# Two orders changed in a hybrid trunk kernel: weight blocks ahead of x's tiles in round 1, the bank ahead of its copy in output pair 1

## The chip, the cores and the metric

The kernel runs on one core of a Trainium2 chip. The metric is the device time of one launch in microseconds (us). Three runs of the kernel before gave a median of 867.38 us, 866.9 to 867.75. The engines are TensorE (PE), VectorE (DVE), ScalarE (ACT), GpSimd (POOL) and SyncE (SP), which issues most of the DMAs.

## The reference

One decoder layer. 2048 rows of x and 16 learned rows, 1024 wide, are normalised; one projection gives eight groups of 512 columns; four feed a gated short convolution, four a chunked retention with four heads; both halves are multiplied by an output matrix, added to the input rows and normalised again.

```python
def mixer_layer(h, norm_g, w_in, conv_w, ret_norm_g, w_out, pos):
    hn = rms_norm(h, norm_g)
    proj = jnp.einsum('bld,de->ble', hn, w_in)
    cx, cb, cc, cg, q, k, v, rg = jnp.split(proj, N_PROJ, axis=-1)
    conv_out = short_conv_branch(cx, cb, cc, conv_w) * jax.nn.silu(cg)
    qf = rotary(q.reshape(shp), pos) * (RET_HEAD_DIM ** -0.5)
    kf, vf = rotary(k.reshape(shp), pos), v.reshape(shp)
    ret = head_group_norm(retention_chunkwise(qf, kf, vf), ret_norm_g)
    ret_out = ret * jax.nn.silu(rg)
    mixed = jnp.concatenate([conv_out, ret_out], axis=-1)
    return h + jnp.einsum('ble,ed->bld', mixed, w_out)

h = mixer_layer(concat(meta, x), ...)
return rms_norm(h, final_g)[:, N_META:]
```

## The kernel before

The two large products, x by the input matrix and the mixed rows by the output matrix, are nearly all of PE's work. Each is cut into block products of 128x128 stationary by 128x512 moving. Every fp32 operand is split in two: a rounded high part (`mh` for the moving operand, `wh` for the stationary one), cast by ACT, and the rest (`ml`, `wl`), a subtraction on DVE. `split` (L116) writes this pair of instructions and keeps the last DVE one in `lowered`. A block product is then three matmuls: high by low, low by high, high by high.

A *quad* takes 2 by 2 blocks. `quad` (L235) forms it with seven products of 12 matmuls, 0 to 6, in three PSUM banks, by the recursion that saves one product in eight. Product 0, and then 2, 4 and 6 build up in the first bank, 1 in the second, 3 and 5 in the third. Between products ACT copies a bank to SBUF (`tc`, L253): the first bank after product 0, again after product 2 (this copy is called u2), and the third after product 3. A product that goes on in a copied bank waits for the copy, or for whoever took the bank. The four results are handed to a function `take(i, j, bank, copy)`: (0, 0) after product 1, (1, 1) after 4, (0, 1) after 5, and (1, 0), which has no copy, after 6. The sums of weight blocks that the recursion needs are made by POOL (L128, L131; tiles `sa` and `ra`).

`quad_plain` (L292) forms a quad with eight products and no sums; its matmuls have line L303. It is used at the start of round 1 (the first quad over x's second 1024 rows, beginning near 360 us) and in output pair 0. In round 1 its stationary operands, in the program's wording the weights' blocks, are cast as `mh30` to `mh33`, from `ra`; x's tiles are `mh00` to `mh13` (first half) and `mh70` to `mh73`, cast with a gain (L122, and L123 on DVE), from `x`. `moving` (L177) runs over x's tiles and splits them.

The outputs are made by pairs of 128-row tiles; pairs 1 and up use `quad`. Their `take` (L950) adds the residual rows, which stand in `yo`: with a copy, first `yo += copy` (on DVE in pair 1, on POOL in later pairs), then `yo = bank + yo` on DVE (L961), which is what frees the bank. Then ACT squares and sums the row (L964, L968), POOL multiplies two of the four quarters by the final gain (L972), and when both quarters of a row are there, DVE and POOL form the factor (L339, L342) and ACT and DVE scale (L993, L996).

The instructions of an engine run in the program's order on it. That order is not the source's: a scheduler sets it from the tiles' dependencies and a timing model, and the source steers it by `tc.issue_after(instruction)`, which places what is issued inside it behind that instruction. `queued` (L110) does so for several.

Of the kernel before, what the change touches and what calls it, by code (L numbers as in the profile page):

```python
# [13 lines left out]
ALU = mybir.AluOpType  # L14
# [5 lines left out]
KT = D // P  # L20
# [6 lines left out]
KH = KT // 2  # L27
# [6 lines left out]
FIRST_W, PLAIN_W, B12 = 2, 3, 4  # L34
# [44 lines left out]
def hybrid_trunk(ctx: ExitStack, tc: tile.TileContext, t, out: bass.AP, chunk_decay):  # L79
# [5 lines left out]
    nc = tc.nc  # L85
# [15 lines left out]
    def gen(name="g"):  # L101
        return sb.tile([P, HB + 16], F32, name=name, tag="g", bufs=GEN)[:, : 2 + HB]
# [1 line left out]
    def brief(name="b"):  # L104
        return sb.tile([P, HB + 128], F32, name=name, tag="b", bufs=BRIEF)[:, :HB]

    lowered, third, fifth, given = [None], [None], [None], [None, None]

    @contextmanager
    def queued(instructions):  # L110
        with ExitStack() as order:
            for ins in instructions:
                order.enter_context(tc.issue_after(ins.ins))
            yield

    def split(hi, lo, src, scale=None, eng=nc.vector):  # L116

        if scale is None:
            nc.scalar.copy(out=hi, in_=src)  # L119
            lowered[0] = eng.tensor_tensor(out=lo, in0=src, in1=hi.bitcast(F32), op=ALU.subtract)  # L120
            return
        scaled[0] = nc.scalar.mul(hi, src, scale)  # L122
        nc.vector.scalar_tensor_tensor(  # L123
            out=lo, in0=src, scalar=scale, in1=hi.bitcast(F32), op0=ALU.mult, op1=ALU.subtract
        )

    def add(eng, out, a, b):
        eng.tensor_tensor(out=out, in0=a, in1=b, op=ALU.add)  # L128
# [34 lines left out]
    def operand(i, kt):  # L163
        slot = B12 if i == 7 else i
        hi = sb.tile([P, HB], F32R, name=f"mh{i}{kt}", tag=f"mh{slot}{kt}", bufs=1)
        lo = sb.tile([P, HB], F32R, name=f"ml{i}{kt}", tag=f"ml{slot}{kt}", bufs=1)
        return hi, lo

    def parts(m, i, kt, src, factor=None):
        hi, lo = operand(i, kt)  # L170
        split(hi, lo, src, factor)
        m[i].append((hi, lo))
# [3 lines left out]
    def moving(load, scale=None, after={}, behind={}):  # L176


        m = [[] for _ in range(8)]
        blocks = []  # L180
        for j in range(2):
            for half in range(2):
                for kt in range(KH):
                    k = half * KH + kt
                    blocks.append(load(k, j))
                    with tc.issue_after(behind[j, k]().ins) if (j, k) in behind else nullcontext():
                        parts(m, BLOCK[half][j], kt, blocks[-1], scale(k) if scale else None)
                    after.get((j, k), lambda: None)()
        return m, blocks
# [91 lines left out]
    def plain_part(n, load, slot):  # L281
        a = sb.tile([P, HB], F32, name="ra", tag="ra", bufs=RAW)
        load(a)
        hi, lo = operand(slot, n)
        split(hi, lo, a)
        return a, (hi, lo)

    def plain_parts(loads, slot=PLAIN_W):
        w = {n: plain_part(n, loads[n], slot)[1] for n in (0, 2, 1, 3)}
        return [w[n] for n in range(4)]  # L290
# [167 lines left out]
    def load_x(r):  # L458
        def load(k, j):
            a = gen("x")[:, :HB]  # L460
            if r == 0:
                in_line(a, t["xT"][r, j, k])
            else:
                nc.sync.dma_start(a, t["xT"][r, j, k])
            return a

        return load
# [73 lines left out]
    def w_loads(n):  # L541
        return [lambda a, i=i: nc.sync.dma_start(a, t["w_in"][n, i]) for i in range(4)]
# [384 lines left out]
    def output(pair, m, final_g):  # L927
        d = mixed[pair // 2]
        loads = [
            lambda a, i=i, k=k: nc.sync.dma_start(a.rearrange("p (k c) -> p k c", k=KH), d[pair % 2, i, k])  # L930
            for i in range(2)
            for k in range(2)
        ]
        ys = [[None, None], [None, None]]
        ss = small.tile([P, 2, 3], F32, name="so", tag="so")
        cuts = [1, 1]
        for i in range(2):
            for j in range(2):
                y = gen("yo")[:, :HB]
                row = (2 * pair + i) * P  # L940
                nc.sync.dma_start(y, x[row : row + P, j * HB : (j + 1) * HB])
                ys[i][j] = y
        last = [None]
        squares = []

        def square():
            while squares:
                squares.pop(0)()

        def take(i, j, pp, c):  # L950
            y = ys[i][j]
            if c is not None:

                with tc.issue_after(fifth[0].ins) if pair == 1 and i + j == 0 else nullcontext():
                    add(nc.vector if pair == 1 else nc.gpsimd, y, y, c)
            junk = sb.tile([P, HB], F32, name="rot", tag="rot", bufs=1)

            cut = 2 if c is None and pair == SEQ // (2 * P) - 1 else 1
            for n in range(cut):
                cs = slice(n * HB // cut, (n + 1) * HB // cut)  # L960
                last[0] = nc.vector.tensor_tensor(out=y[:, cs], in0=pp[:, cs], in1=y[:, cs], op=ALU.add)  # L961
                at = ss[:, i, 2 * n : 2 * n + 1] if i != j and n else ss[:, i, j : j + 1]
                if pair and i + j == 0:
                    squares.append(lambda cs=cs, at=at: nc.scalar.activation(  # L964
                        junk[:, cs], y[:, cs], AF.Square, accum_out=at
                    ))
                else:
                    nc.scalar.activation(junk[:, cs], y[:, cs], AF.Square, accum_out=at)  # L968
            cuts[i] = cut
            if i == j:  # L970
                ys[i][j] = gen("z")[:, :HB]
                nc.gpsimd.tensor_tensor(out=ys[i][j], in0=y, in1=final_g[:, j * HB : (j + 1) * HB], op=ALU.mult)  # L972

        if pair == 0:
            w = plain_parts(loads)
            prepared(m, sums_w, (1, 3))
            quad_plain(w, m, take)
            prepared(m, sums_w, (0, 2), held)
        else:
            quad(stationary(load_raw(loads)), m, take, (idle, idle, square))  # L980
        for i in range(2):
            tot = small.tile([P, 1], F32, name="tot", tag="tot")
            add(nc.vector, tot, ss[:, i, 0:1], ss[:, i, 1:2])
            if cuts[i] > 1:
                add(nc.vector, tot, tot, ss[:, i, 2:3])
            rs = small.tile([P, 1], F32, name="rf", tag="rf")
            rsqrt_mean(rs, tot)
            row = (2 * pair + i) * P
            for j in range(2):
                cs = slice(j * HB, (j + 1) * HB)  # L990
                y = ys[i][j]
                if i == j:
                    nc.scalar.mul(y, y, rs)  # L993
                else:
                    with tc.issue_after(last[0].ins):
                        nc.vector.scalar_tensor_tensor(  # L996
                            out=y, in0=y, scalar=rs, in1=final_g[:, cs], op0=ALU.mult, op1=ALU.mult
                        )
                (nc.scalar if i == j and cuts[i] > 1 else nc.sync).dma_start(out[row : row + P, cs], y)
# [39 lines left out]
    for r in range(NR):  # L1039
# [7 lines left out]
        if r == 0:  # L1047
            w = [[None] * 4 for _ in range(2)]

            def begin(half):  # L1050
                if half:
                    for q, slot in enumerate((FIRST_W, PLAIN_W)):
                        for n in (1, 3):
                            w[q][n] = plain_part(n, lambda a: in_line(a, t["w_in"][2 * NG + q, n]), slot)
                    return
                for n in (0, 2):
                    fetch(1, n, PIECES[0])
# [17 lines left out]
            pieces = []  # L1075

            def meta_behind():
# [3 lines left out]
            after = {  # L1081
                (0, 0): lambda: (begin(0), split_pieces(0)),
                (0, 1): lambda: split_pieces(1),
                (0, KH - 1): lambda: begin(1),
                (0, KT - 1): lambda: (pieces.append(scaled[0]), meta_behind()),
            }
            m, b = moving(load_x(r), gain_of, after, {(0, k): lambda k=k: pieces[k > 1] for k in range(1, KH)})
            first = [[p for a, p in tiles] for tiles in w]
            blocks = None, meta_products([a for a, p in w[0]])
            with tc.issue_after(line[0].ins):  # L1090
# [26 lines left out]
            between = (), idle, idle, idle  # L1117
            later = prepare(load_x(1), sums_x, gain_of)
        else:
            m, b = moving(load_x(r), gain_of)  # L1120
            first = [plain_parts(w_loads(0))]
            load_tables()
            prepared(m, sums_x, (1, 3))

# [12 lines left out]
        for n, unit in enumerate(units):  # L1137
# [10 lines left out]
            else:  # L1148
                if r == NR - 1 and following is None:
                    lent = sb.tile([P, 2, BLK], F32, name="held", tag="rot_t", bufs=1)  # L1150
                    areas = [lent[:, 0], lent[:, 1], row_tile("held", 0), row_tile("held", 0)]
                    for i, a in enumerate(areas):
                        for j in range(2):
                            n, kt = 2 * (i // 2), i % 2 * 2 + j
# [7 lines left out]
    m, b = moving(load_w_out)  # L1162
# [42 lines left out]
```

## Time and profile before

| | |
|---|---|
| median of 3 runs | 867.38 us (866.9 to 867.75) |
| the profiled run's own time | 867.37 us |
| span of the profiled execution | 865.6 us |
| granted TensorE clock, mean | 0.997 of full speed |
| busy: PE, DVE, ACT, POOL | 854.3, 719.0, 499.1, 373.2 us |
| share of PE on the chain that ended last | 86% |

The span is what the trace covers. The run's own time is 1.77 us longer, which is what lies around it. The matmul at L246 alone, three forms of 1008, is 73% of the chain that ended last.

### The profile page before, as it was taken

Reading aid. Unit: us, or ns where it says so; the run is one execution under the profiler, and the core shown is the slowest. Engines: PE = TensorE matmul, PEld = TensorE weight load, DVE = VectorE, ACT = ScalarE, POOL = GpSimd, SP = SyncE. Lnnn points to the kernel's source line nnn. Section 1 sums busy time; section 2 is a strip of 40 time slices with the busy share of each in tenths; the row PEclk is TensorE's granted clock in tenths of the full one; section 3 lists DMA queues with packets and bytes.
Section 4 is the critical chain, followed back from the end, with each engine's and each line's share of the span. In section 5 each row is a group of like instructions: output and inputs, shape, how many; then the busy total and the mean of one; then the engine's idle time right before and its main releaser. Section 6 shows DMA issues by size and latency. Waiting matters only on the chain.

```text
span 865.6 us, 12697 instructions
## 1 busy us (share of the span) xinstructions
PE 854.3 (99%) x4216; PEld 705.0 (81%) x4216; DVE 719.0 (83%) x1204; ACT 499.1 (58%) x901; POOL 373.2 (43%) x278
## 2 busy tenths in 40 slices
PE   9999999999999999999999999999999999999996
PEld 6778888878887778788888888888888888788885
DVE  7788989888897977989789898988767799877663
ACT  8775648474855554948374757544433566545553
POOL 0023232423245554352242323354746555678773
PEclk9999999999999999999999999999999999999998
DMA  9714245454656633845263746646122484545431
GB/s 326 252 62 98 61 97 161 112 146 135 158 173 192 195 98 98 320 142 147 62 158 122 164 129 127 202 114 216 49 77 82 175 324 136 168 164 185 151 135 73
DMA packets 127506, 129.51 MB, mean 150 GB/s; under 512 B 58384, under 2 KB 76112, under 8 KB 127440
## 3 DMA queue, kind: packets, MB, share of 16 engines
q1 hardware_dynamic: 126864, 128.30, 49.7%
q8 instruction: 33, 0.54, 0.3%
q10 hardware_dynamic: 576, 0.40, 0.1%
q14 instruction: 33, 0.27, 0.1%
HBM read 90.91 MB, written 25.17 MB: 134 GB/s over the span
## 4 chain that ended last, share of the span: by engine, by line
PE 86%; DVE 6%; issue 2%; ACT 0%; POOL 0%; POOLq 0%; DVEq 0%
PE pj L246 73%; PE pj L303 5%; PE ms L886 2%; PE ms L875 2%; PE ms L885 2%; PE ms L862 2%; DVE wl L120 1%; PE ms L500 1%; DVE ml L120 1%; DVE yo L128 0%; DVE ml L123 0%; DVE yo L961 0%; PE pj L327 0%; DVE yo L996 0%; ACT n L442 0%
## 5 line engine op out<-in xcount | busy, mean ns | idle before, releaser
L246 PE MATMUL pj<-mh,wl 128*128 128x512 f32 x1008 | 395.9, 393 | 1.6 <-DVE wl L120 1.1
L246 PE MATMUL pj<-mh,wh 128*128 128x512 f32 x1008 | 393.2, 390 | 0.0
L246 PE MATMUL pj<-ml,wh 128*128 128x512 f32 x1008 | 392.7, 390 | 0.0
L119 ACT CAST wh<-ra 128x512 fp32r<-128x512 f32 x216 | 134.0, 620 | 232.5 <-PE pj L246 193.3
L120 DVE TENSOR_TENSOR wl<-ra,wh 128x512 fp32r<-128x512 f32 x216 | 192.4, 893 | 40.8 <-ACT wh L119 39.9
L246 PEld LDWEIGHTS pj<-mh,wl 128*128 128x128 f32 x1008 | 189.3, 188 | 43.1 <-issue 2.3
L246 PEld LDWEIGHTS pj<-mh,wh 128*128 128x128 f32 x1008 | 189.3, 188 | 39.5
L246 PEld LDWEIGHTS pj<-ml,wh 128*128 128x128 f32 x1008 | 189.3, 188 | 38.1
L131 POOL TENSOR_TENSOR ra<-ra 128x512 f32<-128x512 f32 x70 | 115.1, 1644 | 101.6 <-PE ms L500 51.3
L128 POOL TENSOR_TENSOR sa<-ra 128x512 f32<-128x512 f32 x35 | 52.7, 1505 | 102.3 <-DVE wl L120 39.8
L131 POOL TENSOR_TENSOR ra<-sa,ra 128x512 f32<-128x512 f32 x35 | 49.9, 1425 | 81.3 <-DVE wl L120 74.1
L253 ACT COPY tc<-pj 128x512 f32<-128x512 f32 x108 | 62.6, 580 | 0.1
L898 POOL TENSOR_TENSOR rp<-rs,neg_half 128x4 f32<-128x4 f32 x16 | 18.9, 1183 | 45.0 <-DVE rs L128 44.9
L961 DVE TENSOR_TENSOR yo<-pj,yo 128x512 f32<-128x512 f32 (+1 forms) x33 | 22.0, 671 | 16.2 <-PE pj L246 8.1
L972 POOL TENSOR_TENSOR z<-yo,final_g 128x512 f32<-128x512 f32 x16 | 26.8, 1674 | 18.6 <-DVE yo L961 18.6
L647 POOL TENSOR_TENSOR c<-c,rr 128x512 f32<-128x512 f32 x14 | 25.0, 1789 | 21.1 <-DVE c L688 11.1
L119 ACT CAST wh<-sa 128x512 fp32r<-128x512 f32 x36 | 22.2, 618 | 17.4 <-PE pj L246 17.1
L647 POOL TENSOR_TENSOR c<-c,tc 128x512 f32<-128x512 f32 x14 | 23.2, 1659 | 19.9 <-ACT tc L673 19.7
L128 DVE TENSOR_TENSOR tc<-pj,tc 128x512 f32<-128x512 f32 x28 | 19.2, 684 | 13.5 <-PE pj L246 13.3
L902 DVE TENSOR_SCALAR pm<-ms,mv,rp 128x128 f32<-128x128 f32 x64 | 21.8, 402 | 10.2 <-POOL rp L898 10.2
L123 DVE SCALAR_TENSOR_TENSOR ml<-x,gain,mh 128x512 fp32r<-128x512 f32 x32 | 25.2, 822 | 5.5 <-ACT mh L122 5.4
L120 DVE TENSOR_TENSOR wl<-sa,wh 128x512 fp32r<-128x512 f32 x36 | 28.9, 804 | 0.8 <-ACT wh L119 0.7
(161 smaller groups left out, 1256.0 us busy)
## 6 DMA issues: line engine op xcount, KB each, us to landing
ra<-in_w_in SPq DMA_DIRECT2D x124, 256.0 KB, 2.8
x<-in_xT SPq DMA_DIRECT2D x48, 256.0 KB, 4.9
w<-in_w_out SPq DMA_DIRECT2D x32, 256.0 KB, 4.5
ra<-mixed SPq DMA_DIRECT2D x32, 256.0 KB, 2.7
yo<-in_x SPq DMA_DIRECT2D x32, 256.0 KB, 4.9
ra<-in_x SPq DMA_DIRECT2D x16, 256.0 KB, 3.4
mixed<-c SPq DMA_DIRECT2D x16, 256.0 KB, 2.4
sums_x<-x SPq DMA_DIRECT2D x16, 256.0 KB, 2.8
```

The lines of the kernel that those rows point to most:

```text
L119: nc.scalar.copy(out=hi, in_=src)
L120: lowered[0] = eng.tensor_tensor(out=lo, in0=src, in1=hi.bitcast(F32), op=ALU.subtract)
L123: nc.vector.scalar_tensor_tensor(out=lo, in0=src, scalar=scale, in1=hi.bitcast(F32), op0=ALU.mult, op1=ALU.subtract)
L128: eng.tensor_tensor(out=out, in0=a, in1=b, op=ALU.add)
L131: eng.tensor_tensor(out=out, in0=a, in1=b, op=ALU.subtract)
L246: nc.tensor.matmul(bank, a[:, ks], b, start=first and kt == 0 and n == 0, stop=kt == KH - 1 and n == 2, skip_group_check=not first,)
L253: copied[0] = nc.scalar.copy(out=c, in_=bank)
L303: nc.tensor.matmul(banks[i], a[:, ks], b, start=half + kt + n == 0, stop=half == 1 and kt == KH - 1 and n == 2,)
L647: eng.tensor_tensor(out=out, in0=a, in1=b, op=ALU.mult)
L902: nc.vector.tensor_scalar(out=y[:, cs], in0=o[:, cs], scalar1=mv[:, c, 0:1], scalar2=rp[:, c, :], op0=ALU.subtract, op1=ALU.mult,)
L961: last[0] = nc.vector.tensor_tensor(out=y[:, cs], in0=pp[:, cs], in1=y[:, cs], op=ALU.add)
L972: nc.gpsimd.tensor_tensor(out=ys[i][j], in0=y, in1=final_g[:, j * HB : (j + 1) * HB], op=ALU.mult)
```

## The change

Two things are edited.

First, in round 1. Before, all of x's tiles were split (`moving`), and then the weights' four blocks. Now the parts of blocks 0 and 2 are written behind x's first tile, those of 1 and 3 behind its third, and every x tile but the first is queued behind the last cast and the last subtraction of the weight blocks. `split` keeps the cast in `raised` for that.

Second, in output pair 1, for the two quarters (1, 1) and (0, 1), which have a copy: `yo = bank + yo` comes first and `yo += copy` second. Quarter (0, 0) and all other pairs are as before. No operation is added or removed.

```diff
-    lowered, third, fifth, given = [None], [None], [None], [None, None]
+    lowered, raised, third, fifth, given = [None], [None], [None], [None], [None, None]
...
         if scale is None:
-            nc.scalar.copy(out=hi, in_=src)
+            raised[0] = nc.scalar.copy(out=hi, in_=src)
             lowered[0] = eng.tensor_tensor(out=lo, in0=src, in1=hi.bitcast(F32), op=ALU.subtract)
...
                     blocks.append(load(k, j))
-                    with tc.issue_after(behind[j, k]().ins) if (j, k) in behind else nullcontext():
+                    with queued(behind.get((j, k), list)()):
                         parts(m, BLOCK[half][j], kt, blocks[-1], scale(k) if scale else None)
...
             y = ys[i][j]
-            if c is not None:
+            late = pair == 1 and c is not None and i + j > 0
+            if c is not None and not late:
...
                 last[0] = nc.vector.tensor_tensor(out=y[:, cs], in0=pp[:, cs], in1=y[:, cs], op=ALU.add)
+                if late:
+                    last[0] = nc.vector.tensor_tensor(out=y, in0=y, in1=c, op=ALU.add)
...
-            m, b = moving(load_x(r), gain_of)
-            first = [plain_parts(w_loads(0))]
+            loads, w = w_loads(0), {}
+
+            def begin(ns):
+                for n in ns:
+                    w[n] = plain_part(n, loads[n], PLAIN_W)[1]
+
+            m, b = moving(
+                load_x(r), gain_of, {(0, 0): lambda: begin((0, 2)), (0, 2): lambda: begin((1, 3))},
+                {(j, k): lambda: [raised[0], lowered[0]] for j in range(2) for k in range(KT) if j + k},
+            )
+            first = [[w[n] for n in range(4)]]
             load_tables()
```

ACT at the start of round 1, before. `mh30` and its fellows are the weights' blocks, `mh00` to `mh13` x's tiles, `wh` a weight of the quad that runs before, `rr` row factors.

```order
L122 ACTIVATE mh10_3838<-x_3836,gain_69 128x512 [waits DMAHW6_49]
L119 CAST wh_3670<-ra_3639 128x512 [waits DVE_49,PE_49]
L253 COPY tc_3747<-pj_3678 128x512
L673 ACTIVATE tc_3691<-tc_3691 128x512 [waits DVE_49]
L122 ACTIVATE mh11_3844<-x_3842,gain_69 128x512 [waits DMAHW7_49]
L376 COPY rr_2929<-ms_3699 128x512 [waits PE_49]
L378 ACTIVATE rr2_2930<-ms_3699 128x512
L119 CAST mh30_3910<-ra_3908 128x512 [waits PE_49]
L122 ACTIVATE mh12_3850<-x_3848,gain_69 128x512 [waits DMAHW0_49]
L119 CAST mh31_3922<-ra_3920 128x512 [waits PE_49]
L122 ACTIVATE mh13_3856<-x_3854,gain_69 128x512 [waits DMAHW1_49]
L119 CAST mh32_3916<-ra_3914 128x512 [waits PE_49]
```

The same place now:

```order
L119 CAST wh_3666<-ra_3641 128x512 [waits PE_49,Activation_49]
L119 CAST wh_3670<-ra_3639 128x512 [waits DVE_49,PE_49]
L253 COPY tc_3747<-pj_3678 128x512
L673 ACTIVATE tc_3691<-tc_3691 128x512 [waits DVE_49]
L376 COPY rr_2929<-ms_3699 128x512 [waits PE_49]
L378 ACTIVATE rr2_2930<-ms_3699 128x512
L119 CAST mh30_3820<-ra_3818 128x512 [waits DMAHW6_49,PE_49]
L119 CAST mh31_3844<-ra_3842 128x512 [waits DMAHW0_49,PE_49]
L119 CAST mh32_3826<-ra_3824 128x512 [waits DMAHW7_49,PE_49]
L122 ACTIVATE mh01_3832<-x_3830,gain_69 128x512 [waits DMAHW3_49]
L122 ACTIVATE mh02_3838<-x_3836,gain_69 128x512 [waits DMAHW4_49]
```

The weights' casts moved ahead of x's tiles `mh01` to `mh11`.

DVE in output pair 1, before. `yo_7386` is quarter (1, 1), `tc_7489` its copy, `pj_7429` the first bank, `wl_7426` the low part that product 6 needs.

```order
L120 TENSOR_TENSOR wl_7422<-ra_7390,wh_7421 128x512 [waits Activation_49]
L128 TENSOR_TENSOR yo_7382<-yo_7382,tc_7474 128x512 [waits DMAHW2_49,Activation_49]
L120 TENSOR_TENSOR wl_7426<-ra_7394,wh_7425 128x512 [waits DMAHW4_49,Activation_49]
L128 TENSOR_TENSOR yo_7386<-yo_7386,tc_7489 128x512 [waits DMAHW4_49,Activation_49]
L961 TENSOR_TENSOR yo_7386<-pj_7429,yo_7386 128x512 [waits DVE_49,PE_49]
L120 TENSOR_TENSOR wl_7580<-ra_7570,wh_7579 128x512 [waits DMAHW3_49,Activation_49]
L961 TENSOR_TENSOR yo_7382<-pj_7476,yo_7382 128x512 [waits PE_49]
```

And now:

```order
L120 TENSOR_TENSOR wl_7422<-ra_7390,wh_7421 128x512 [waits Activation_49]
L120 TENSOR_TENSOR wl_7426<-ra_7394,wh_7425 128x512 [waits DMAHW4_49,Activation_49]
L962 TENSOR_TENSOR yo_7386<-pj_7429,yo_7386 128x512 [waits DMAHW4_49,PE_49]
L120 TENSOR_TENSOR wl_7580<-ra_7570,wh_7579 128x512 [waits DMAHW3_49,Activation_49]
L964 TENSOR_TENSOR yo_7386<-yo_7386,tc_7489 128x512 [waits DVE_49]
L962 TENSOR_TENSOR yo_7382<-pj_7476,yo_7382 128x512 [waits DMAHW2_49,PE_49]
```

Both additions of a copy moved behind the addition of the bank.

PE in the next pair, 2, whose source is not edited: the first rows of products 2, 3 and 4, before. `mh20` marks product 2, `mh30` product 3, `mh40` product 4; `pj_7611` is the first bank, `pj_7658` the third.

```order
L246 MATMUL pj_7611<-mh20_7165,wl_7592 128x512 [waits DVE_49,Activation_49]
L246 MATMUL pj_7611<-ml20_7166,wh_7591 128x512
...
L246 MATMUL pj_7658<-mh30_7327,wl_7596 128x512 [waits DVE_49]
L246 MATMUL pj_7658<-ml30_7328,wh_7595 128x512
...
L246 MATMUL pj_7611<-mh40_7343,wl_7600 128x512 [waits DVE_49,Activation_49]
```

And now:

```order
L246 MATMUL pj_7658<-mh30_7327,wl_7596 128x512 [waits DVE_49]
L246 MATMUL pj_7658<-ml30_7328,wh_7595 128x512
...
L246 MATMUL pj_7611<-mh20_7165,wl_7592 128x512 [waits Activation_49]
L246 MATMUL pj_7611<-ml20_7166,wh_7591 128x512
...
L246 MATMUL pj_7611<-mh40_7343,wl_7600 128x512 [waits DVE_49,Activation_49]
```

The scheduler has exchanged products 2 and 3, 12 matmuls each. ACT there, before and now, `tc_7656` being u2 of the first bank:

```order
L119 CAST wh_7603<-ra_7572 128x512 [waits DVE_49,PE_49]
L253 COPY tc_7656<-pj_7611 128x512
L119 CAST wh_7607<-ra_7576 128x512 [waits DMAHW0_49,DVE_49,PE_49]
L253 COPY tc_7671<-pj_7658 128x512
```

```order
L119 CAST wh_7603<-ra_7572 128x512 [waits DVE_49,PE_49]
L119 CAST wh_7607<-ra_7576 128x512 [waits DMAHW0_49,PE_49]
L253 COPY tc_7656<-pj_7611 128x512
L253 COPY tc_7671<-pj_7658 128x512
```

The cast of `wh_7607` moved ahead of the copy u2.

## Rows read from the trace of the kernel before

**Rows 1.** The page's part 1: busy us, share of the span, instructions.

```profile
PE 854.3 (99%) x4216; PEld 705.0 (81%) x4216; DVE 719.0 (83%) x1204; ACT 499.1 (58%) x901; POOL 373.2 (43%) x278
```

**Rows 2.** PE's waits: us in total, times, longest us.

```profile
PE pj L303 <- DVE ml L120: 1.0, 1, 1.0
...
PE pj L246 <- DVE yo L961: 0.5, 1, 0.5
```

**Rows 3.** Timeline of PE near 361 us: start, duration, instruction, [idle <-releaser].

```profile
360.00 0.39 PE L303 MATMUL pj<-mh,mh 128*128 128x512 f32 x1
361.40 0.50 PE L303 MATMUL pj<-mh,ml 128*128 128x512 f32 x1 [1.01 <-DVE ml L120]
```

**Rows 4.** Timeline of ACT, 353 to 359 us.

```profile
353.12 2.70 ACT L122 ACTIVATE mh<-x,gain 128x512 fp32r<-128x512 f32 x4 [0.39 <-DMA x<-in_xT]
...
357.25 0.71 ACT L122 ACTIVATE mh<-x,gain 128x512 fp32r<-128x512 f32 x1
...
358.81 0.62 ACT L119 CAST mh<-ra 128x512 fp32r<-128x512 f32 x1
```

**Rows 5.** Timeline of DVE, 354 to 361 us.

```profile
354.51 0.67 DVE L647 TENSOR_TENSOR tc<-tc,rr 128x512 f32<-128x512 f32 x1
...
360.67 0.68 DVE L120 TENSOR_TENSOR ml<-ra,mh 128x512 fp32r<-128x512 f32 x1
```

**Rows 6.** Timeline of DVE, 388 to 404 us, three of 18 rows.

```profile
388.70 0.69 DVE L709 TENSOR_TENSOR rot<-kv,rot_t 64x512 f32<-64x512 f32 x1 [2.27 <-ACT kv L766]
...
401.60 1.78 DVE L712 TENSOR_TENSOR qg<-qg,rot 128x512 f32<-128x512 f32 x1
403.31 0.68 DVE L128 TENSOR_TENSOR qg<-pj,tc 128x512 f32<-128x512 f32 x1
```

**Rows 7.** Timeline of PE at product 6 of the next quad.

```profile
404.83 0.39 PE L246 MATMUL pj<-mh,wl 128*128 128x512 f32 x1
```

**Rows 8.** Timeline of POOL, 382 to 403 us.

```profile
382.36 5.23 POOL L131 TENSOR_TENSOR ra<-ra 128x512 f32<-128x512 f32 x1 [6.02 <-issue]
387.55 1.28 POOL L647 TENSOR_TENSOR c<-c,tc 128x512 f32<-128x512 f32 x1
401.39 1.45 POOL L128 TENSOR_TENSOR sa<-ra 128x512 f32<-128x512 f32 x1 [12.55 <-DMA ra<-in_w_in]
```

**Rows 9.** Timeline of PE near 741 us, output pair 1.

```profile
740.34 0.39 PE L246 MATMUL pj<-mh,wh 128*128 128x512 f32 x1
741.24 0.50 PE L246 MATMUL pj<-mh,wl 128*128 128x512 f32 x1 [0.51 <-DVE yo L961]
741.57 0.39 PE L246 MATMUL pj<-ml,wh 128*128 128x512 f32 x1
```

**Rows 10.** Timeline of DVE, 739 to 741 us.

```profile
739.11 0.68 DVE L120 TENSOR_TENSOR wl<-ra,wh 128x512 fp32r<-128x512 f32 x1
739.71 0.68 DVE L128 TENSOR_TENSOR yo<-yo,tc 128x512 f32<-128x512 f32 x1
740.49 0.69 DVE L961 TENSOR_TENSOR yo<-pj,yo 128x512 f32<-128x512 f32 x1
```

**Rows 11.** Timeline of PE in pair 2: product 2's last matmul, first ones of 3 and 4.

```profile
752.02 0.39 PE L246 MATMUL pj<-mh,wh 128*128 128x512 f32 x1
752.25 0.39 PE L246 MATMUL pj<-mh,wl 128*128 128x512 f32 x1
...
754.97 0.39 PE L246 MATMUL pj<-mh,wl 128*128 128x512 f32 x1
```

**Rows 12.** Timeline of ACT behind product 2 of pair 2.

```profile
752.45 0.62 ACT L119 CAST wh<-ra 128x512 fp32r<-128x512 f32 x1 [2.10 <-PE pj L246]
752.98 0.58 ACT L253 COPY tc<-pj 128x512 f32<-128x512 f32 x1
```

**Rows 13.** Timeline of DVE, 748 to 752 us: a scaling, then product 3's low part.

```profile
748.93 1.87 DVE L996 SCALAR_TENSOR_TENSOR yo<-yo,rf,final_g 128x512 f32<-128x512 f32 x1 [0.66 <-POOL rf L342]
750.72 0.68 DVE L120 TENSOR_TENSOR wl<-sa,wh 128x512 fp32r<-128x512 f32 x1
```

More of the change, by code (lines that the diff above doesn't have):

```diff
@@ L1086, in hybrid_trunk @@
             }
-            m, b = moving(load_x(r), gain_of, after, {(0, k): lambda k=k: pieces[k > 1] for k in range(1, KH)})
+            m, b = moving(load_x(r), gain_of, after, {(0, k): lambda k=k: [pieces[k > 1]] for k in range(1, KH)})
             first = [[p for a, p in tiles] for tiles in w]
```

## The prediction

> **What bounds the kernel now.** I read the busy shares first: PE works 854.3 us of 865.6, 99%, and no other engine comes near [rows 1]. So a change pays only where PE waits, and costs only where it makes PE wait. The view of PE's waits comes second: behind the opening stretch, two of them are over 0.2 us, one at L303 for a subtraction and one at L246 for an addition of pair 1 [rows 2]. They are where the two edits apply. The timelines of PE then give what each takes. Matmuls start every 0.227 us when nothing holds them (12 of them from 752.25 to 754.97 [rows 11]).
>
> At 361.40 the start is 1.40 us behind the one before it, so 1.17 is lost [rows 3]; at 741.24 it is 0.90, so 0.67 is lost, and the matmul behind it starts 0.33 later and not 0.227, which is 0.11 more [rows 9]. I count this restart of 0.11 with every wait. Together, 1.28 + 0.78 = 2.06 us is the most that can be gained. That is 0.24% of the time; about 0.2%, 1.74 us, is what a measurement of this kernel can tell from no change.
>
> **Round 1, the wait itself.** No operation is added; the order on ACT changes. PE's matmul at 361.40 needs the low part that DVE begins at 360.67 [rows 5], and that one needs the cast that ACT begins at 358.81 [rows 4]. Before it ACT does five tiles of x (four at 353.12, one at 357.25) in the same stretch. Now none of them is between `wh_3670` and the first weight. What remains is bound by DVE: the row factor is multiplied at 354.51, ending 355.18 [rows 5], and behind it on ACT come the activation L673, two factor rows and the cast, at 0.5 us from one to the next (the cast of 752.45 is followed after 0.53 [rows 12]). The cast starts near 355.2 + 3 x 0.53 = 356.8, 2.0 us sooner, and the low part ends near 358.2 where PE wants it at 360.23. The other three weights follow at some 0.6 us each. The wait goes, with 2 us to spare, and so 1.28 us.
>
> **Round 1, what is late next.** PE now runs 1.28 us ahead, but DVE has the same operations to do. The place to look is where DVE has no gap: from 388.70 to 403.31 it works without one, through 18 rows [rows 6]. The last of these, `qg<-pj,tc` of the next quad, frees the first bank for product 6, which starts at 404.83 [rows 7]. It ends 403.31 + 0.68 = 403.99, so PE has 0.84 us to spare there. The chain starts at 388.70, behind ACT's copy of a bank of PE's, after 2.27 us of idle time. If it starts 1.28 sooner like PE, the margin stays and place one is worth the whole 1.28. If DVE's own backlog holds the start at 388.70, product 6 is 1.28 - 0.84 = 0.44 late, with the restart 0.55, and 0.73 is left. If one more meeting with POOL falls on the busy stretch, then 1.09 more (the op at 401.60 took 1.78 where its like takes 0.69 [rows 6], under POOL's addition from 401.39 to 402.84 [rows 8]): stall 1.64, and place one loses 0.36. The reason to expect something of that kind is that POOL's operation of 387.55 lies in DVE's idle time now [rows 6, 8]; when everything of PE's comes 1.28 sooner, that idle time shrinks to about 1.0 us and does not cover its 1.28. Against it, the meeting of 401.39 can move ahead of the chain's end without changing its cost. Laid out with the rows' durations, the new order has the chain start between 387.6 and 388.9; at the middle, 388.3, it is 0.4 sooner, and product 6 is 1.28 - 0.84 - 0.4, about nothing, late. With half a meeting to a whole one (0.55 to 1.09) and the restart that is 0.7 to 1.2. I take the middle, 0.94: place one is **-0.34**, between -1.28 and +0.36.
>
> The Trainium skill ("SBUF — State Buffer", section "Who interferes with whom") calls the port pair of DVE and GpSimd an exclusive lock, and says that whoever starts first holds it for the whole instruction. The 1.78 at 401.60 fits that; POOL's 5.23 us at 382.36, where DVE kept on issuing, shows POOL waiting through several of DVE's instructions rather than one [rows 8]. [...]
>
> **Pair 1.** The bank that product 6 waits for is freed at 741.18 by L961 (740.49 + 0.69), in front of which stands `yo<-yo,tc` of 739.71 [rows 10]. Now that addition comes behind. Even with the low part left at 739.11, L961 starts at 739.71 and ends 740.40, before 740.34 + 0.227 = 740.57, when PE is ready. The wait of 0.78 us goes: **-0.78**. The additions that are put later have the same length and DVE has idle time behind them; POOL and ACT get the quarter (1, 1) later, but PE does not wait for it.
>
> **Pair 2, which nobody edited.** The scheduler exchanges products 2 and 3. Product 4 goes on in product 2's bank, and must wait for the copy u2 of it. Before, product 3's 12 matmuls (2.72 us [rows 11]) stood between, and cast and copy were hidden: behind product 2's last matmul at 752.02 the cast starts at 752.45, the copy at 752.98, and it ends 753.56, well before 754.97 [rows 11, 12]. Now product 4 is next in PE's order, the cover is gone, and the cast of `wh_7607` stands ahead of the copy on ACT. From the last matmul to the first of product 4 it takes 753.56 - 752.02 = 1.54, plus about 0.05 for the signal, 1.59 in place of 0.227: 1.36, with the restart **+1.47**. Lower bound, if the copy goes first: without the cast's 0.53 it is 0.94. Upper bound: an ACT scaling or square in front, some 0.7 more, 2.2.
>
> Product 3 now also starts one product sooner, where product 2 starts now: 752.25 - 2.72 = 749.53, less 0.78 is 748.75. Its low part began at 750.72 before, behind a scaling of 1.87 us that met POOL [rows 13]. In the new order the two scalings stand directly in front of it. Their inputs come 0.78 sooner, with PE. Without the meeting (1.87 to 0.75, 1.1 less) the low part starts at 750.72 - 0.78 - 1.1 = 748.84; the sum and the factor of the second row now stand ahead of both scalings, which I put at 0.6 more; with its own 0.68 it ends at 748.9. That is 0.15 late, with the restart 0.26; between 0 and 1.4 (if the meeting remains). I take **+0.2**. Behind this PE has no wait to the end that could take the loss up, so pair 2 costs 1.67.
>
> **The sum.** -0.34 - 0.78 + 1.47 + 0.2 = +0.55. On the profiled run's own 867.37 us (its span of 865.6 with 1.77 around it, and the same as the median of 867.38) this is **867.9 us**. The rest of the edits (where DMAs of the weights stand against x's on SP, the later square of one quarter) I set at nothing: PE reads none of their results within 2 us.
>
> **The rivals.**
>
> *A. Both waits go and nothing new appears.* -2.06, 865.3 us. For it: both waits are real, and in the first place the margin is 2 us. Against: the exchange in pair 2 has a price read from rows, and the hardware keeps the order of each engine.
>
> *B. DVE falls behind and the bank comes late, slower than before.* Mechanism: PE's lead at 361 pulls POOL's operations onto DVE's busy stretch, DVE's chain to 403.99 gets one meeting more, and product 6 waits 1.64 us; in pair 2 the same happens in front of product 3's low part (+1.4 in place of 0.2). Sum: +0.36 - 0.78 + 1.47 + 1.4 = +2.45, 869.8 us; with the first alone +1.25, 868.6. It is measurably slower from about 1.7 us lost beyond the gain, which needs the second meeting nearly whole. For it: the 1.09 us of each meeting is in the rows; against: POOL must hit these places.
>
> *C. Round 1 keeps its whole 1.28.* DVE's chain starts as much sooner as PE. -1.28 - 0.78 + 1.67 = -0.39, 867.0 us. For it: DVE's idle 2.27 is larger than 1.28.
>
> *D. The edit in round 1 does nothing*, because the weights' tiles or a DMA hold the cast where it was. 0 - 0.78 + 1.67 = +0.9, 868.3 us. Against: ACT runs without a gap there.
>
> **How the numbers follow.** Forecast 0.48 (867.3 to 868.5), C 0.20, B 0.18, D 0.07, A 0.07. Only A with all of its 2.06 is faster by over 0.2%: 0.07. Slower needs +1.74: the upper part of B, 0.14, and 0.02 of the forecast with an upper bound on u2. Within 0.2%: 0.77. The range of 8 in 10 runs from C with the copy first (-0.9, 866.5) to B (869.2).
>
> **What would show it.** Round 1: no wait at the second L303 matmul, and the first weight's cast near 356.8. If product 6 of the next quad is not late, C holds; if it is late by over 1.5, B. Pair 1: no wait for L961 at product 6. Pair 2: a wait at the first matmul of product 4, released by ACT's copy at L253, of about 1.3 us idle between starts; and a short one, or none, at product 3. The forecast is wrong if there is no wait for L253, or if the new PE wait near 405 exceeds one microsecond.

## The result and the profile after

Measured: 869.35 us, median of 7 runs (868.35 to 871.03), against 867.36 us (866.38 to 867.75) of the kernel before. The ratio is 1.0028, 95% interval 1.0018 to 1.0037. The change makes the kernel 1.99 us slower. The forecast was 867.9 us with a range that ended at 869.2.

PE's waits in the trace after (us in total, times, longest us):

```profile
PE pj L246 <- DVE wl L120: 2.1, 4, 0.9
PE pj L246 <- DVE qg L128: 1.4, 1, 1.4
PE pj L246 <- ACT tc L253: 1.2, 1, 1.2
```

Both waits of [rows 2] that the edits aim at are gone. Two lines are new, one for DVE's `qg` and one for ACT's copy, and the waits for weights' low parts have grown (1.1 us before, over the whole run).

The profiled run is the slowest of the seven, 871.03 us, so its span of 869.2 must not be compared with 865.6 as it stands. It is read by stage: the lag of one matmul of PE behind the same one in the trace of before. The rows of after, in order of time:

```profile
361.54 0.39 PE L303 MATMUL pj<-mh,mh 128*128 128x512 f32 x1
361.76 0.39 PE L303 MATMUL pj<-mh,ml 128*128 128x512 f32 x1
...
404.83 0.39 PE L246 MATMUL pj<-mh,wh 128*128 128x512 f32 x1
406.61 0.50 PE L246 MATMUL pj<-mh,wl 128*128 128x512 f32 x1 [1.39 <-DVE qg L128]
...
750.60 0.39 PE L246 MATMUL pj<-mh,wh 128*128 128x512 f32 x1
751.53 0.50 PE L246 MATMUL pj<-mh,wl 128*128 128x512 f32 x1 [0.54 <-DVE wl L120]
...
756.92 0.39 PE L246 MATMUL pj<-mh,wh 128*128 128x512 f32 x1
758.50 0.50 PE L246 MATMUL pj<-mh,wl 128*128 128x512 f32 x1 [1.19 <-ACT tc L253]
```

| matmul | before | after | lag |
|---|---|---|---|
| first at L303 | 360.00 [rows 3] | 361.54 | 1.54 |
| second at L303 | 361.40 [rows 3] | 361.76 | 0.36 |
| product 6 of the next quad | 404.83 [rows 7] | 406.61 | 1.78 |
| first of the second product in pair 2 | 752.25 - 2.72 = 749.53 [rows 11] | 751.53 | 2.00 |
| product 4 of pair 2 | 754.97 [rows 11] | 758.50 | 3.53 |

The first 1.54 us lie ahead of both edits, where PE's matmuls are the same in both kernels: it is the variation of the opening from run to run. In e1 (below), which has the same edit there, this matmul starts at 359.64, 0.36 earlier than before. From there to product 4 the lag grows by 3.53 - 1.54 = 1.99 us, as much as the difference of the medians (2.12 with the restart behind that wait). So the loss lies at the places of the table: -1.18 at 361 us, +1.42 to product 6, +0.22 to pair 2 (in it pair 1's gain, the wait in front of product 3, a restart and some 0.2 at other places), then +1.53.

The wait at 361 is gone because ACT casts the first three weights from 358.34 on, with no tile of x ahead of them ([rows 4] had five in the same stretch):

```profile
357.85 0.61 ACT L378 ACTIVATE rr<-ms 128x512 f32<-128x512 f32 x1
358.34 1.67 ACT L119 CAST mh<-ra 128x512 fp32r<-128x512 f32 x3
```

358.34 - 1.54 is 356.80 on the clock of before, where the prediction put it.

At product 6 the chain on DVE is the cause. POOL and then DVE in the trace after, up to 406 us; they answer to [rows 6, 8]:

```profile
401.66 1.44 POOL L128 TENSOR_TENSOR sa<-ra 128x512 f32<-128x512 f32 x1 [18.46 <-DMA ra<-in_w_in]
403.18 1.63 POOL L131 TENSOR_TENSOR ra<-ra 128x512 f32<-128x512 f32 x1
```

```profile
390.33 0.69 DVE L709 TENSOR_TENSOR rot<-kv,rot_t 64x512 f32<-64x512 f32 x1
...
401.25 0.69 DVE L120 TENSOR_TENSOR wl<-ra,wh 128x512 fp32r<-128x512 f32 x1
401.86 1.79 DVE L711 TENSOR_TENSOR qg<-qg,rot_t 128x512 f32<-128x512 f32 x1
403.57 1.79 DVE L120 TENSOR_TENSOR wl<-ra,wh 128x512 fp32r<-128x512 f32 x1
405.28 0.68 DVE L712 TENSOR_TENSOR qg<-qg,rot 128x512 f32<-128x512 f32 x1
405.88 0.68 DVE L128 TENSOR_TENSOR qg<-pj,tc 128x512 f32<-128x512 f32 x1
```

Two DVE operations take 1.79 us instead of 0.69, one under each of POOL's. Before, only one meeting, at 401.60, stood ahead of the addition that frees the bank. POOL starts when a DMA of weights lands; on the clock of before that is now 401.66 - 1.54 = 400.12 and not 401.39, so the second of POOL's operations comes sooner too and meets a subtraction ahead of the addition. Before, it began at 402.92 (1.63 us long) and met the addition itself, which took its usual 0.68 [rows 6].

I added up DVE's 65 operations from the multiplication by the row factor ([rows 5], 354.51; 356.05 after) to that addition, up to its start. They are the same instructions in both kernels, in another order:

| | from, to | length | idle | operations lengthened by POOL | their excess |
|---|---|---|---|---|---|
| before | 354.51, 403.31 | 48.80 | 2.27 | 6 | 5.83 |
| after | 356.05, 405.88 | 49.83 | 1.07 | 8 | 7.92 |

(The excess is what an operation takes over 0.68 us, or over 0.74 where it works on a tile of x.) The bare work is 40.7 and 40.8. DVE's idle time of 2.27 us was not free time: POOL worked in it, and with PE ahead POOL works beside busy DVE. Two meetings more take 2.1 us. And 1.07 us of idle time is new, at another place: the subtractions of x's tiles that DVE did there before now stand behind the weights, and DVE waits for ACT's cast of the first weight.

```profile
359.00 1.90 DVE L120 TENSOR_TENSOR ml<-ra,mh 128x512 fp32r<-128x512 f32 x3 [1.07 <-ACT mh L119]
```

Every kernel with round 1's edit has this wait, of 1.07 or 1.72 us; no kernel without it has.

In pair 2, ACT behind product 2 of the trace after (answers to [rows 12]):

```profile
757.34 0.62 ACT L119 CAST wh<-ra 128x512 fp32r<-128x512 f32 x1 [2.09 <-PE pj L246]
757.87 0.58 ACT L253 COPY tc<-pj 128x512 f32<-128x512 f32 x1
```

The copy ends at 758.45 and product 4 starts at 758.50: 1.58 us after the last matmul in front of it; 1.59 was forecast.

### The profile page after: what moved, and what is told of

The parts are those of the page before. It is cut to its first block, busy times and chain, and to the rows that moved or that the text cites. A ratio compares the mean times of both kernels' runs of the same rounds, so it can differ in the third digit from the quotient of the medians.

```text
span 869.2 us, 12709 instructions
## 1 busy us (share of the span) xinstructions
PE 855.8 (98%) x4216; PEld 705.4 (81%) x4216; DVE 707.9 (81%) x1204; ACT 498.9 (57%) x901; POOL 372.2 (43%) x278
## 5 line engine op out<-in xcount | busy, mean ns | idle before, releaser
L246 PE MATMUL pj<-mh,wl 128*128 128x512 f32 x1008 | 396.2, 393 | 4.7 <-DVE wl L120 2.1
L246 PE MATMUL pj<-mh,wh 128*128 128x512 f32 x1008 | 393.2, 390 | 0.0
L246 PE MATMUL pj<-ml,wh 128*128 128x512 f32 x1008 | 392.8, 390 | 0.0
L246 PEld LDWEIGHTS pj<-mh,wl 128*128 128x128 f32 x1008 | 189.3, 188 | 47.3 <-issue 2.3
L120 DVE TENSOR_TENSOR wl<-ra,wh 128x512 fp32r<-128x512 f32 x216 | 189.5, 880 | 45.2 <-ACT wh L119 44.2
L246 PEld LDWEIGHTS pj<-mh,wh 128*128 128x128 f32 x1008 | 189.3, 188 | 39.5
L246 PEld LDWEIGHTS pj<-ml,wh 128*128 128x128 f32 x1008 | 189.3, 188 | 37.8
L131 POOL TENSOR_TENSOR ra<-ra 128x512 f32<-128x512 f32 x70 | 109.8, 1569 | 99.8 <-PE ms L500 51.7
L123 DVE SCALAR_TENSOR_TENSOR ml<-x,gain,mh 128x512 fp32r<-128x512 f32 x32 | 27.3, 888 | 5.9 <-ACT mh L122 5.8
L128 POOL TENSOR_TENSOR yo<-yo,tc 128x512 f32<-128x512 f32 x18 | 28.4, 1578 | 8.6 <-ACT tc L253 8.6
```

Of the source, the lines that this page charges most:

```text
L123: nc.vector.scalar_tensor_tensor(out=lo, in0=src, scalar=scale, in1=hi.bitcast(F32), op0=ALU.mult, op1=ALU.subtract)
L131: eng.tensor_tensor(out=out, in0=a, in1=b, op=ALU.subtract)
L246: nc.tensor.matmul(bank, a[:, ks], b, start=first and kt == 0 and n == 0, stop=kt == KH - 1 and n == 2, skip_group_check=not first,)
```

## The experiments

Theory: round 1's loss is DVE's two additional meetings with POOL ahead of product 6, and pair 2's loss is the exchange of two products. Rival at first: the loss belongs to one of the edits as a whole, or to the opening. Each edit is shown against the changed kernel, with what is left out marked; line numbers shift with the edits (L252 in e6 is L246 here). "Gap" below is the time from one matmul's start to the next, 0.23 where nothing holds it. Every kernel was timed against the kernel before on the same chip; the median of before was 867.54 us beside e1 to e4, 867.23 beside e6, e7, e9 and e10, and 867.00 beside e8, e11 and e10 again.

| run | what it is | median, us | ratio to before, 95% interval |
|---|---|---|---|
| e1 | round 1 alone | 868.02 | 1.0006 (0.9997 to 1.0015) |
| e2 | pair 1 alone | 868.96 | 1.0019 (1.0010 to 1.0028) |
| e3 | pair 1, products kept in order | 868.45 | 1.0007 (0.9998 to 1.0016) |
| e4 | round 1, rotary behind the addition | 867.50 | 1.0002 (0.9992 to 1.0011) |
| e6 | round 1, POOL held back | 865.84 | 0.9988 (0.9980 to 0.9997) |
| e7 | pair 1, u2 ahead of the cast | 868.73 | 1.0016 (1.0007 to 1.0026) |
| e8 | both edits, POOL held back | 867.60 | 1.0004 (0.9995 to 1.0012) |
| e9 | pair 1, quarter (1, 1) alone | 867.49 | 1.0005 (0.9996 to 1.0014) |
| e10 | e6 and e9 together | 865.86 | 0.9982 (0.9974 to 0.9991) |
| e10 again | the same | 866.62 | 0.9997 (0.9988 to 1.0006) |
| e11 | e10, scaling behind the copy | 865.28 | 0.9980 (0.9971 to 0.9989) |

**e1, e2: each edit alone.**

```diff
-            late = pair == 1 and c is not None and i + j > 0
+            late = False
```

```diff
-            loads, w = w_loads(0), {}
...
-            first = [[w[n] for n in range(4)]]
+            m, b = moving(load_x(r), gain_of)
+            first = [plain_parts(w_loads(0))]
```

The first is e1's, the second e2's; e3, e7 and e9 have the second too.

> Only the edit in round 1; output pair 1 as before. Theory: the wait at 361 us goes (-1.28 us) and product 6 of the next quad waits instead, 1.55 us plus the restart of 0.11 as in the changed kernel, so +0.4 us, 867.7 us; PE's waits name DVE qg at L128 (1.4 us idle), the wait for yo in pair 1 (0.5) is still there, none for ACT's copy at L253. Rival: the changed kernel's loss comes from round 1 as a whole (its profile is already 1.4 us behind at 357 us): then this kernel takes nearly all of it, 869 us.

> Only the edit in output pair 1. Theory: the wait for yo in pair 1 goes (-0.78 us), products 2 and 3 of pair 2 are exchanged, product 3 waits for its low part (0.70 + 0.11) and product 4 for the copy u2 (1.36 + 0.11): +1.5 us, 868.9 us, and the wait at 361 us is still there. Rival (pair 2 costs little, the loss is round 1's): 866.6 to 867.4 us.

PE's waits in e1, three of the lines:

```profile
PE pj L246 <- DVE qg L128: 1.4, 1, 1.4
...
PE pj L246 <- DVE wl L120: 0.6, 2, 0.5
PE pj L246 <- DVE yo L962: 0.5, 1, 0.5
```

The wait for `qg` is there with round 1's edit alone (gap 1.79), the one at 361 is gone, and the time is 0.5 us above before: as the theory has it, though the interval includes no change. e2 has PE's products 2 and 3 exchanged, the gap of 1.58 in front of product 4, and 1.4 us more time, with an interval that leaves out no change. One thing of the theory failed there: in front of product 3 the gap is only 0.40 in e2. In e7, whose order is the same up to there, it is 0.82, in e8 0.94. In e2 PE had waited before, at 697.10 (gap 0.60), where the changed kernel, e7 and e8 have no wait; with the restart that is 0.5 us, about what product 3 waits less. That the one made up for the other fits the numbers and was not tested. Neither edit holds the whole loss, and the two medians' differences, 0.48 and 1.42, add up to 1.90 of the 1.99.

**e3, e9, e7: why pair 2 loses.** e3 queues product 3 behind product 2, so PE's order is that of before:

```diff
         product(2, xb, False)
+        second = last_mm[0]
...
-        product(3, zb, True)
+        with tc.issue_after(second.ins) if pinned else nullcontext():
+            product(3, zb, True)
...
```

> Only the edit in output pair 1, and in pair 2 product 3 is queued behind product 2, so that PE's order is that of before. Theory: only the gain is left, -0.78 us, 866.6 us, with no wait of PE in pairs 1 and 2. Rival (the moved additions themselves delay DVE, and product 3's or 4's operands come late in any order): a wait of PE for wl in pair 2, 867.4 us or more.

My theory failed; the rival was right that PE waits in pair 2 in any order, though the wait is not for a low part. PE waits one product earlier; PE and ACT of e3:

```profile
749.20 0.39 PE L246 MATMUL pj<-mh,wh 128*128 128x512 f32 x1
750.46 0.50 PE L246 MATMUL pj<-mh,wl 128*128 128x512 f32 x1 [0.87 <-ACT tc L253]
```

```profile
748.08 0.73 ACT L998 ACTIVATE z<-z,rf 128x512 f32<-128x512 f32 x1 [0.83 <-POOL rf L344]
748.71 0.60 ACT L119 CAST wh<-sa 128x512 fp32r<-128x512 f32 x1
749.22 0.72 ACT L998 ACTIVATE z<-z,rf 128x512 f32<-128x512 f32 x1
749.84 0.56 ACT L253 COPY tc<-pj 128x512 f32<-128x512 f32 x1
```

Product 2 needs the copy of product 0's bank. On ACT that copy stands behind two scalings of pair 1, the first of which waits for POOL's factor. The late addition of quarter (0, 1) puts the sums and factors later and both scalings ahead of the copy. So without the exchange of products PE waits for this copy; that the scheduler exchanged them to go around it is likely, and not shown.

e9 makes only quarter (1, 1) late:

```diff
-            late = pair == 1 and c is not None and i + j > 0
+            late = pair == 1 and c is not None and i + j > 1
```

> Only the edit in output pair 1, and there for quarter (1, 1) alone; (0, 1) adds its copy first, as before. PE's order is then that of before, and on ACT the copy of pair 2's product 0 stands ahead of the second scaling again. Theory (the loss in pair 2 comes from the late addition of quarter (0, 1), which makes the sums, the scalings and the copy later): the wait for yo goes (-0.78 us) and no wait of PE in pair 2 comes: 866.7 us. Rival (any late addition costs pair 2 its copy): a wait for ACT's copy at L253 of about 1 us, 867.8 us.

```profile
749.76 0.50 PE L246 MATMUL pj<-mh,wl 128*128 128x512 f32 x1 [0.40 <-ACT tc L253]
```

The theory failed here too. The products are not exchanged, and only one scaling is ahead of the copy, but a gap of 0.79 in front of product 2 stays, released by the same copy. The wait for `yo` is gone, and 0.67 of its 0.78 us are given back 8 us later. The time does not differ from before. So the rival holds in kind: what PE gains in pair 1 it loses in pair 2, as long as the copy stands behind a scaling whose factor comes later.

e7 leaves the products exchanged and puts the cast behind u2, the only change of order against e2:

```diff
...
         u2 = copy(xb)
+        if callable(w[6]):
+            with tc.issue_after(copied[0].ins):
+                w[6] = w[6]()
```

> Only the edit in output pair 1, with products 2 and 3 of pair 2 exchanged as there, but the cast for product 6 stands behind the copy u2 on ACT. Theory: the gap in front of product 4 falls by the cast's 0.53 us, from 1.58 to 1.05 us from start to start, still a wait for ACT's copy. Rival (the copy waits for something else than the cast ahead of it): the gap stays 1.58.

```profile
754.33 0.39 PE L248 MATMUL pj<-mh,wh 128*128 128x512 f32 x1
755.39 0.50 PE L248 MATMUL pj<-mh,wl 128*128 128x512 f32 x1 [0.68 <-ACT tc L255]
```

The gap is 1.06 instead of 1.58: the cast ahead of the copy is 0.52 of the price, the missing cover of product 3 the rest.

**e4, e6, e8: what holds product 6.** e4 puts the rotary of the first query half behind the addition that frees the bank:

```diff
+                if r == 1 and h == 0 and j == 0:
+                    return
...
+                    freed = nc.vector.tensor_tensor(out=d, in0=pp, in1=c, op=ALU.add)
+                    if r == 1 and h == 0:
+                        with tc.issue_after(freed.ins):
+                            rotary(q[0], tables[0])
...
```

> Only the edit in round 1, and in the next quad (query and gate of head 0) the rotary of the first query half stands behind the addition that frees product 6's bank. Theory: DVE reaches that addition some 2.7 us sooner (four operations of about 0.7 us), more than the 1.55 us that product 6 was late, so no wait near 405 us: -1.28 us, 866.1 us. Rival (DVE is behind as a whole): the wait moves to the next bank that DVE frees, and the time stays near 867.5 us.

```profile
419.61 0.39 PE L246 MATMUL pj<-mh,wh 128*128 128x512 f32 x1
420.75 0.49 PE L892 MATMUL ms<-v,pm 128*128 128x128 f32 x2 [0.75 <-DVE pm L884]
```

No wait near 405, and a new one of 0.91 (1.14 - 0.23) at 420, for another DVE operation. That is the rival in kind: it named a bank that DVE frees, and PE waits for an operand that DVE makes. Moving DVE's work here only moves the place.

e6 leaves the order on every engine as in e1 and holds POOL back. A copy of one column that reads the query half after its rotary stands ahead of the two additions on POOL; it is the only instruction in which the two traces differ:

```diff
+        if later is not None:
+            gate = nc.gpsimd.tensor_copy(out=small.tile([P, 1], F32, name="gate", tag="gate", bufs=1), in_=later[:, :1])
+        with tc.issue_after(gate.ins) if gate else nullcontext():
             add(eng, s1, a21, a22)
             sub(eng, a21, a11, a21)
...
```

> Only the edit in round 1, and POOL's two block additions of the next weights (at 401.7 and 403.2 us in the changed kernel) are held back by a tiny POOL copy that reads the query half after its rotary, so that they run once DVE has reached the addition that frees product 6's bank; the orders of the other engines are those of the kernel with round 1's edit alone. Theory (the stall near 405 is made by DVE's meetings with POOL): both meetings of 1.1 us go from DVE's chain, which then ends about 2.2 us sooner, before PE wants the bank: no wait there. What of the 1.28 us is kept depends on whether DVE is late again behind it (near 420, as in the run with the rotary moved). 866.3 if not, 867.3 if so. Rival (DVE's own backlog, POOL does not matter): the wait of 1.4 us idle near 405 stays, 867.9 us.

POOL and DVE of e6:

```profile
402.90 0.19 POOL L157 COPY gate<-qg 128x1 f32<-128x1 f32 x1 [20.60 <-DVE qg L718]
403.04 1.30 POOL L128 TENSOR_TENSOR sa<-ra 128x512 f32<-128x512 f32 x1
404.42 1.62 POOL L131 TENSOR_TENSOR ra<-ra 128x512 f32<-128x512 f32 x1
```

```profile
400.95 0.68 DVE L717 TENSOR_TENSOR qg<-qg,rot_t 128x512 f32<-128x512 f32 x1
401.55 0.68 DVE L120 TENSOR_TENSOR wl<-ra,wh 128x512 fp32r<-128x512 f32 x1
402.16 0.68 DVE L718 TENSOR_TENSOR qg<-qg,rot 128x512 f32<-128x512 f32 x1
402.76 0.68 DVE L128 TENSOR_TENSOR qg<-pj,tc 128x512 f32<-128x512 f32 x1
403.47 1.42 DVE L812 TENSOR_TENSOR qg<-qg,rr 128x512 f32<-128x512 f32 x1
404.81 1.78 DVE L120 TENSOR_TENSOR wl<-ra,wh 128x512 fp32r<-128x512 f32 x1
```

```profile
403.93 0.39 PE L252 MATMUL pj<-mh,wh 128*128 128x512 f32 x1
404.16 0.39 PE L252 MATMUL pj<-mh,wl 128*128 128x512 f32 x1
```

The operations of 1.79 ahead of the addition are back at 0.68. DVE's excess over the 65 operations is 5.70 instead of 7.92, its chain 47.61 us long instead of 49.83, and PE goes through product 6 (404.16) without a wait. The two meetings now stand behind the addition, and near 420 the largest gap is 0.31, which with its restart gives 0.2 us back. So in this trace round 1's edit keeps 1.1 of its 1.28 us once POOL is held. The time is 1.39 us below before, and the interval just leaves out no change. This shows the two meetings, and not DVE's own work, to be the cause of the wait at product 6. The Trainium skill ("SBUF — State Buffer", section "Who interferes with whom") says that a DVE instruction with two inputs in SBUF contends with a GpSimd instruction that reads SBUF, and that one with at most one such input, outside the modes that use both ports, does not. The trace agrees: the addition at 402.76, which reads one of its inputs from PSUM, took its 0.68 us beside POOL's operation of 403.04, and that one its 1.30.

e8 is the changed kernel with the same hold:

> The changed kernel as it is, with POOL's two additions held back in round 1. Theory (the 1.66 us near 405 is from those two meetings alone, and pair 2's loss stands by itself): 869.35 - 1.66 = 867.7 us, the same as before within what can be measured, no wait near 405, the gap of 1.58 us in front of product 4 of pair 2 still there. Rival (the losses in pair 2 are DVE's lateness carried on from round 1): the waits in pair 2 go too, 866.0 us or less.

```profile
753.88 0.39 PE L252 MATMUL pj<-mh,wh 128*128 128x512 f32 x1
755.46 0.50 PE L252 MATMUL pj<-mh,wl 128*128 128x512 f32 x1 [1.20 <-ACT tc L259]
```

It takes 867.6 us; 867.7 was expected. That is 0.6 above before, and the interval includes no change. The gap of 1.58 stands, so pair 2's loss is not lateness carried on from round 1 (the wait in front of product 3 stands there too, 0.94 from start to start).

**e10, e11: a version below both kernels.** e10 joins e6 and e9:

> Both edits, with POOL's two additions held back in round 1 and the late addition for quarter (1, 1) alone. Theory: no wait at 361, none at 405, none for yo, none in pair 2: 867.4 - 1.28 - 0.78 = 865.3 us if nothing comes near 420, 866.3 if the wait there comes. Rival (DVE takes all back in round 1): 867.4 - 0.78 + 0.4 = 867.0 us.

It was timed twice: 1.4 us below before, with an interval that leaves out no change, and then 0.4 below (e10 again), with one that includes it. No wait stands at 361 or 405 in either trace, and the gap in pair 2 stays, 0.79 and 0.83. e11 also puts pair 1's scalings behind the copy of pair 2's product 0:

```diff
+        def finish_pair():
+            while rest_of_pair:
+                y, rs, row, cs = rest_of_pair.pop(0)
+                nc.scalar.mul(y, y, rs)
+                nc.sync.dma_start(out[row : row + P, cs], y)
...
-            quad(stationary(load_raw(loads)), m, take, (idle, idle, square))
+            quad(stationary(load_raw(loads)), m, take, (finish_pair, idle, square))
```

> The best version so far (both edits, POOL's two additions held back in round 1, the late addition for quarter (1, 1) alone), and in addition pair 1's first scaling on ACT stands behind the copy of pair 2's product 0; nothing else changes its place. Theory (pair 2's product 2 waits because the copy stands on ACT behind a scaling that waits for POOL's factor): the gap of 0.79 us in front of product 2 goes, so 0.67 us less than without, 865.2 us against 865.9. Rival (the copy is late for another reason, the square or the cast in front of it): the gap stays, no difference.

> The best version so far once more, beside the one with the scaling moved, so that the two can be compared on one chip: 865.9 us, with the gap of 0.79 us in front of product 2 of pair 2.

ACT of e11, and all of PE's waits there:

```profile
745.42 0.58 ACT L259 COPY tc<-pj 128x512 f32<-128x512 f32 x1
745.90 0.72 ACT L963 ACTIVATE z<-z,rf 128x512 f32<-128x512 f32 x1
```

```profile
PE ms L1046 <- DVE warm L1038: 1.0, 1, 1.0
PE pj L252 <- DVE wl L120: 0.5, 1, 0.5
PE ms L381 <- DVE rot L355: 0.3, 1, 0.3
```

That scaling's place is the only difference to e10 in the order of any engine. The scaling is behind the copy, the gap is gone, and at the places of this study only a gap of 0.39 near 420 is left. The time is 865.28 us, 1.7 below before, and the interval leaves out no change. Beside e10 again, on the same chip, it is 1.34 us lower; the trace accounts for 0.67 of that, the wait that is gone, and the two intervals still touch.

## Why the prediction was wrong

The forecast was a loss of 0.55 us; 1.99 was measured. Two terms of its sum were too small, place one in round 1 (-0.34, measured +0.38) and product 3 in pair 2 (+0.2, measured +0.81). Together they are 1.33 of the 1.44 us that were missing. One of the prediction's own signs of being wrong came: the new wait near 405 is 1.39 us, over one microsecond.

- **What bounds it, and the two waits: right.** Both went, for the reasons given, the cast at 356.80 on the clock of before.
- **Round 1, what is late next: the place and the mechanism right, the size wrong.** The term was -0.34, with +0.36 as the worst. From the gaps it is -1.28 + (1.78 - 0.23) + 0.11 = +0.38, just past the worst end. The prediction let DVE's chain start 0.4 us sooner and gave it half a meeting to a whole one. In fact the second rotary started at 390.33 - 1.54 = 388.79, no sooner than 388.70: of the idle time there before, 1.07 us went to the wait for ACT's cast at 359.00, which the prediction does not name, and about 1.0 to one more meeting with POOL (six up to there, five before). Then another one more stood ahead of the addition. e6 shows that without the two meetings there PE does not wait.
- **The place of 401.39: a false step.** The prediction said that POOL's meeting "can move ahead of the chain's end without changing its cost". The operation behind it on POOL moved along, and its meeting cost 1.1 us more.
- **Pair 1: right, -0.78,** but it was not to be had alone: the copy in pair 2 had too little to spare, and in e3, e9 and e10 PE waited there for it; only in e11 did it not.
- **The copy u2: right,** 1.58 - 0.23 + 0.11 = +1.46 against +1.47, and e7 shows the split into cast and cover.
- **Product 3: too small,** +0.2 against 0.93 - 0.23 + 0.11 = +0.81. Here the working does not add up: a start at 748.84, 0.6 more and the operation's own 0.68 end at 750.12 and not at 748.9. That is 1.37 late, +1.48 with the restart, and would have made the forecast 869.2 us. It would have come near by luck, this term too large and round 1's too small. In the trace the two scalings take their usual 0.7 each, as forecast, and the low part ends at 751.47, 0.64 after PE could have started. Ahead of it stand a meeting of 1.59 us (a subtraction at 744.48), then `yo += copy` of quarter (0, 1), the sums and the factors. The size is not fixed: in e2 the gap is 0.40.

The sum of the measured terms, 0.38 - 0.78 + 1.46 + 0.81 = +1.87, is close to the 1.99 measured. It is rival B, which had 0.18, with its first part as priced and its second at 0.81 in place of 1.4. For round 1 the forecast took between half a meeting more and a whole one; the trace has two more, one up to the second rotary and one behind it.

## What to carry to other kernels

Where one engine gains time, look for idle time of a second engine in which a third did its work: that idle time is not slack, and its cost appears as soon as the first engine runs ahead. Before a reordering is priced, read the new order of every engine also behind the edit: the scheduler may exchange work there, and pinning the old order need not help, as in e3, where PE waited one product earlier instead. A wait that is only moved can come back at the next place, as it did in e3, e4 and e9; here it went where its cause was taken away, in e6 by holding POOL off DVE and in e11 by putting the copy ahead of the scalings that made it late.

## What had not been expected of the hardware

The opening of a run differs by up to 2.2 us between the thirteen traces, in the same matmuls of PE: the one that starts at 300.70 before, ahead of both edits, starts between 300.02 (e10 again) and 302.24 (after). For e10, traced twice, it is 300.58 and 300.02. 2.2 us is 0.26% of the time, so effects of this size are compared stage by stage and not by the spans of two profiles.

And a POOL operation that meets a run of DVE work can cost DVE nothing or 1.1 us. Before, the one at 382.36 took 5.23 us [rows 8], with DVE's operations at their usual length; after, the same operation started at 381.58 and took 1.62, and the DVE operation of 381.97 took 1.77. By the records POOL's started 0.22 and 0.21 us behind the start of a DVE subtraction (382.14 and 381.37), so that alone does not tell the two cases apart. What does stays open.
